# Attention on one core: ten key tiles one by one, or in five pairs, with the pair buffers in the space of W_o

## The chip, the cores and the metric

The kernel runs on one core of a Trainium2 chip. The metric is the device time of one execution in microseconds (us), as the median of the runs. Before the change three runs gave 2367.48, 2368.72 and 2373.99 us; the median is 2368.72 us.

## The reference, cut to what matters

The program is a two-layer diffusion backbone over 1024 latent tokens of width 1024. Layer 0 is grouped-query attention and a mixture of experts, layer 1 a Fourier mixer and a mixture of experts, and a final norm follows. The change touches the attention core alone:

```
k_all = concat([k_latent, k_context])            # 1024 + 256 keys
s = einsum('bqkgd,bskd->bkgqs', q, k).astype(f32) * ATTN_SCALE
p = softmax(s, axis=-1)
o = einsum('bkgqs,bskd->bqkgd', p, v)            # then o @ w_o
```

There are 16 query heads of 64, 4 key heads, and 4 query heads to a key head.

## The kernel before, in words

`phase_qkv` projects, normalises and rotates queries, keys and values. Queries lie in DRAM (`QS`), keys (`KS`, and `KL` with the low halves and two rows of ones) and values (`V`) in SBUF. `phase_attn` (L617) then works through 16 units; a unit is half of the queries (512) for one pair of heads. `phase_wo` applies W_o, and the experts follow.

`main` (L643) does one unit. For each of the ten key tiles (`kt`, 128 keys) it computes the scores of two heads: for each head one product of `KS` with `qs` (L658) and one of `KL` with `qm` (L659), which subtracts the row maximum. The scores (`st`, in PSUM, two buffers) go through the exponential on ScalarE (L673) into a tile `pe` (four buffers of 128x1024). GpSimd adds up the `pe` tiles for the softmax denominator (L680 for the first two, then L684). TensorE multiplies `pe` with V (`pv`, L664; four instructions, two for each head, each head in its own half of the output partitions), one key tile behind the scores, and accumulates in `po`. At the end ScalarE copies `po` out (L703).

Three kinds of other work are threaded in between, each as a list from which `main` pops steps:

- `fill`: the row maxima of the next unit (`smax_steps`, L548). 24 steps are a product (L561, of 512, 512 and 256 keys in turn, into two PSUM buffers `sm`) and its maximum on VectorE (L562). Then `negate` reduces, casts and subtracts on VectorE (L571, L573, L574). `fin`, always the last, transposes the result on TensorE (L581) and ScalarE copies it into `qm` (L582), which the next unit's scores need. `maxima()` pops one step, three times in each key tile, and never pops `fin`, which is popped after `pv` of tile 8.
- `tail`: the end of the unit before: `total` (four products of the sum with ones, L715, copied by L716 into `su`), four reciprocals on VectorE (L719), and `scale` (L722). One step is popped in each key tile from the third on.
- `ada`: modulation vectors of later stages. A step loads 1 MB of weights (L190, on SP's queue) and multiplies it (L245, eight instructions in four column groups of 32). It is popped in key tiles 2, 5 and 8 (`ADA_AT`), for 45 steps in all.

TensorE's instructions keep the order of the program in this phase (`manual_schedule` for PE alone). The instructions of the other engines are ordered by the planner of the framework, by its own times; a step whose inputs are ready can go ahead of its place in the program. Each engine and SP's queue then run strictly in that order.

Ahead of unit 15 (`WO_AT`) the first two quarters of W_o are loaded and split (L740: `split_piece` casts on ScalarE, L200, and subtracts on VectorE, L201) into the four 8 KB buffers of pool `wowA` (two named `wh`, two `wl`). Until then `wowA` is unused in this phase. Unit 15 has no next unit, so its `fill` is empty.

The main loop, cut:

```
for kt in range(NTA):
    scores(ps, kt, 0); maxima(); scores(ps, kt, 1)
    pe = pp.tile([P, 2, 512], F32, name="pe")
    nc.scalar.activation(pe, ps, AF.Exp, scale=SCALE)
    ...                                   # GpSimd adds pe to acc
    maxima()
    if prev is not None:
        pv(*prev)
    prev = (kt, pe)
    maxima()
    ...                                   # fin, tail, ada
pv(*prev)
```

Of the kernel before, what the change touches and what calls it, by code (L numbers as in the profile page):

```python
# [10 lines left out]
F32 = mybir.dt.float32  # L11
# [3 lines left out]
AF = mybir.ActivationFunctionType  # L15
# [5 lines left out]
P = 128  # L21
# [4 lines left out]
NTA = (SEQ + CTX) // P  # L26
# [14 lines left out]

LAG = 2
WQ_AT = 6
ADA_AT = (2, 5, 8)
SUM_DVE = (7, 8, 9)
WO_AT = 15

# [23 lines left out]
SCALE = HD ** -0.5  # L71
# [467 lines left out]
def load_queries(g, u, pool):  # L539

    hf, pr = u
    qs = pool.tile([P, 2, 512], F32R, name="qs")
    g.qs_load = g.nc.sync.dma_start(qs.bitcast(F32),
                                    g.QS[2 * pr:2 * pr + 2, :, hf * 512:(hf + 1) * 512].rearrange("h p t -> p h t"))
    return qs


def smax_steps(g, u, qs, wk, pp, tag, tagt, bufs=None):  # L548


    nc = g.nc
    hf, pr = u
    g4 = pr // 2
    m3 = g.atq.tile([P, 2, 4, 3], F32, name="m3")
    todo = []
    for h in range(2):
        for qt in range(4):
            for b, (k0, kn) in enumerate(((0, 512), (512, 512), (1024, 256))):
                def f(h=h, qt=qt, b=b, k0=k0, kn=kn):
                    ps = pp.tile([P, 512], F32, name=tag)  # L560
                    nc.tensor.matmul(ps[:, :kn], qs[:, h, qt * P:(qt + 1) * P], g.KS[:, g4, k0:k0 + kn], start=True, stop=True)  # L561
                    nc.vector.reduce_max(m3[:, h, qt, b:b + 1], ps[:, :kn], axis=AX.X)  # L562
                todo.append(f)
    qm = wk.tile([66, 2, 512], F32R, name="qm", bufs=bufs)
    nc.sync.dma_start(qm[:64].bitcast(F32), g.QS[2 * pr:2 * pr + 2, 0:64, hf * 512:(hf + 1) * 512].rearrange("h p t -> p h t"))

    box = {}

    def negate():
        nm = g.atq.tile([P, 8], F32, name="nm")  # L570
        nc.vector.tensor_reduce(nm, m3.rearrange("p h q b -> p (h q) b"), axis=AX.X, op=OP.max, negate=True)  # L571
        box["mc"] = mc = g.atq.tile([P, 8, 2], F32R, name="mc")
        nc.vector.tensor_copy(mc[:, :, 0], nm)  # L573
        nc.vector.tensor_sub(mc[:, :, 1], nm, mc[:, :, 0])  # L574

    def fin():
        mc = box["mc"]
        for h in range(2):
            pt = pp.tile([P, 512], F32R, name=tagt)
            for qt in range(4):  # L580
                nc.tensor.transpose(pt[:2, qt * P:(qt + 1) * P], mc[:, h * 4 + qt], g.identr)  # L581
            nc.scalar.copy(qm[64:66, h], pt[:2])  # L582

    todo += [negate, fin]
    return qm, todo
# [31 lines left out]
def phase_attn(g):  # L617
    nc, tc, a = g.nc, g.tc, g.a
    with ExitStack() as st:
        pp = g.pool(st, "atP", 4)  # L620
        wk = g.pool(st, "at", 2)
        third = g.pool(st, "at3", 1)
        p1 = g.pool(st, "at1", 2, psum=True)
        po_ = g.pool(st, "ato", 1, psum=True)
        p2 = g.pool(st, "at2", 2, psum=True)
        units = [(hf, pr) for g4 in range(HKV) for hf in range(2) for pr in (2 * g4, 2 * g4 + 1)]
        state = {}

        def smax(i):
            qm, todo = smax_steps(g, units[i], Q[i], wk, p1, "sm", "sm")  # L630
            state[units[i]] = (Q[i], qm)
            return todo

        def queries(i):

            if i < len(units):
                Q[i] = load_queries(g, units[i], third if i % 3 == 2 else g.atq)

        Q = {}

        tail, ada = [], []

        def main(u, fill):  # L643
            hf, pr = u
            g4 = pr // 2
            qs, qm = state.pop(u)
            po = po_.tile([P, 512], F32, name="po")
            P0 = {}
            prev = None

            def maxima(n=1):

                for _ in range(min(n, len(fill) - 1)):
                    fill.pop(0)()

            def scores(ps, kt, h):
                ks = slice(kt * P, (kt + 1) * P)
                nc.tensor.matmul(ps[:, h], g.KS[:, g4, ks], qs[:, h], start=True, stop=False)  # L658
                nc.tensor.matmul(ps[:, h], g.KL[:, g4, ks], qm[:, h], start=False, stop=True)  # L659

            def pv(kt, pe):

                for h in range(2):
                    nc.tensor.matmul(po[64 * h:64 * h + 64], g.V[:, kt, g4 * HD:(g4 + 1) * HD], pe[:, h],  # L664
                                     start=(kt == 0), stop=(kt == NTA - 1))

            for kt in range(NTA):
                ps = p2.tile([P, 2, 512], F32, name="st")
                scores(ps, kt, 0)
                maxima()  # L670
                scores(ps, kt, 1)
                pe = pp.tile([P, 2, 512], F32, name="pe")
                nc.scalar.activation(pe, ps, AF.Exp, scale=SCALE)  # L673
                side = 0 if u == units[-1] and kt in SUM_DVE else 1
                eng = (nc.vector, nc.gpsimd)[side]
                if side not in P0:
                    P0[side] = pe
                elif not isinstance(P0[side], tuple):
                    acc = wk.tile([P, 2, 512], F32, name=f"acc{side}", bufs=1 + side)
                    eng.tensor_add(acc, P0[side], pe)  # L680
                    P0[side] = (acc,)
                else:
                    acc = P0[side][0]
                    eng.tensor_add(acc, acc, pe)  # L684
                maxima()
                if prev is not None:
                    pv(*prev)
                prev = (kt, pe)
                maxima()
                if kt == NTA - 1 and fill:  # L690
                    fill.pop(0)()
                if kt >= 2 and tail:
                    tail.pop(0)()
                if kt in ADA_AT and ada:
                    ada.pop(0)()
            pv(*prev)
            if u == units[-1]:
                end = g.atq.tile([P, 2, 512], F32, name="qs")
                ou, su = end[:, 0], end[:, 1]
            else:  # L700
                ou = wk.tile([P, 512], F32, name="ou")
                su = wk.tile([P, 512], F32, name="su", bufs=1)
            nc.scalar.copy(ou, po)  # L703
            accP = P0[1][0]
            accD = P0.get(0)
            if isinstance(accD, tuple):
                accD = accD[0]


            def total():  # L710
                if accD is not None:
                    nc.gpsimd.tensor_add(accP, accP, accD)
                ps = p1.tile([P, 512], F32, name="sm")
                for h in range(2):
                    nc.tensor.matmul(ps[64 * h:64 * h + 64], g.ones64, accP[:, h], start=True, stop=True)  # L715
                nc.scalar.copy(su, ps)  # L716

            def inverse(j):
                nc.vector.reciprocal(su[:, j * P:(j + 1) * P], su[:, j * P:(j + 1) * P])  # L719

            def scale():
                nc.vector.tensor_mul(g.X[:, 4 * hf:4 * hf + 4, pr * P:(pr + 1) * P], ou.rearrange("p (t n) -> p t n", t=4),  # L722
                                     su.rearrange("p (t n) -> p t n", t=4))
            tail.extend([total] + [lambda j=j: inverse(j) for j in range(4)] + [scale])

        for l, gi in ((0, 1), (0, 2), (1, 0), (1, 1), (1, 2)):
            steps = adaln_group(g, l, gi, po_, wk, after=not ada)
            ada += steps[:-1]
            ada.append(lambda f=steps[-1], l=l, gi=gi: adaln_store(g, l, gi, f()))
        state[units[0]] = g.smax0  # L730
        queries(1)
        for i, u in enumerate(units):
            queries(i + 2)
            f1 = smax(i + 1) if i + 1 < len(units) else []
            if i == 6:
                with tc.issue_after(g.qs_load.ins):
                    for n, t in g.tab.items():
                        nc.sync.dma_start(t, a["dft_" + n])
            if i == WO_AT:
                g.wo_pieces = [split_piece(g, load_piece(g, a["attn_w_o"][0, i * 256:(i + 1) * 256], 2), g.wowA) for i in range(2)]  # L740
            with tc.manual_schedule(engines={mybir.EngineType.PE}):
                main(u, f1)
        tail.pop(0)()
        g.tail = tail
# [1367 lines left out]
```

## Time and profile before

| what | us |
|---|---|
| median of three runs | 2368.72 |
| the profiled execution | 2366.65 |
| its span, first to last instruction | 2364.70 |
| up to the attention units | about 240 |
| the sixteen units | 240 to 738.6 |
| W_o, routing, first experts' start | 738.6 to 940 |
| the rest | 940 to 2364.7 |

All times in the trace count from the start of the span. PE is TensorE's products, PEld its weight loads, DVE VectorE, ACT ScalarE, POOL GpSimd, SP the queue that issues most transfers. A row of a timeline gives start, length, engine, line, operation, tiles and how many instructions are merged in it; in brackets is how long the engine was idle before it and what ended that.

### The profile page before, as it was taken

Reading aid. Unit: us, or ns where it says so; the run is one execution under the profiler, and the core shown is the slowest. Engines: PE = TensorE matmul, PEld = TensorE weight load, DVE = VectorE, ACT = ScalarE, POOL = GpSimd, SP = SyncE. Lnnn points to the kernel's source line nnn. Section 1 sums busy time; section 2 is a strip of 40 time slices with the busy share of each in tenths; the row PEclk is TensorE's granted clock in tenths of the full one; section 3 lists DMA queues with packets and bytes.
Section 4 is the critical chain, followed back from the end, with each engine's and each line's share of the span. In section 5 each row is a group of like instructions: output and inputs, shape, how many; then the busy total and the mean of one; then the engine's idle time right before and its main releaser. Section 6 shows DMA issues by size and latency. Waiting matters only on the chain. (4 is left out here: it accounts for less than half of the span.)

```text
span 2364.7 us, 29621 instructions
## 1 busy us (share of the span) xinstructions
PE 2149.3 (91%) x10250; PEld 1424.5 (60%) x10250; DVE 1949.1 (82%) x2822; ACT 1338.1 (57%) x1741; POOL 1045.2 (44%) x560
## 2 busy tenths in 40 slices
PE   6899999999999777999999999669699999999993
PEld 3677444444445565677777766447476777776662
DVE  4878566666675788999999999676899999998995
ACT  4733344443444235677776776443476777766773
POOL 2322566676767632334334442443233434423432
PEclk8999999999999898999999999879799999999997
DMA  8544434534333777999999999645599999999995
GB/s 304 186 160 141 165 112 134 180 112 134 115 114 129 255 250 267 359 361 331 353 345 343 362 361 336 213 192 213 218 307 348 339 343 351 354 345 347 348 366 198
DMA packets 152631, 614.22 MB, mean 260 GB/s; under 512 B 26961, under 2 KB 43993, under 8 KB 106461
## 3 DMA queue, kind: packets, MB, share of 16 engines
q1 hardware_dynamic: 110188, 546.87, 63.4%
q0 software_dynamic: 24672, 54.40, 9.0%
q10 hardware_dynamic: 17616, 11.01, 1.5%
q8 instruction: 82, 1.34, 0.2%
q14 instruction: 73, 0.59, 0.1%
HBM read 559.57 MB, written 78.44 MB: 270 GB/s over the span
## 5 line engine op out<-in xcount | busy, mean ns | idle before, releaser
L207 PE MATMUL h<-wl,xh 128*104 128x512 f32 x1024 | 411.6, 402 | 20.2 <-DVE wl L1229 16.9
L206 PE MATMUL h<-wh,xh 128*104 128x512 f32 x1024 | 410.4, 401 | 3.3 <-ACT wh L1224 3.3
L208 PE MATMUL h<-wh,xl 128*104 128x512 f32 x1024 | 406.6, 397 | 0.0
L684 POOL TENSOR_TENSOR acc<-acc,pe 128x1024 f32<-128x1024 f32 x125 | 298.8, 2391 | 96.4 <-ACT pe L673 94.0
L562 DVE TENSOR_REDUCE m<-sm 128x1 f32<-128x512 f32 x360 | 206.3, 591 | 136.4 <-PE sm L561 134.7
L673 ACT ACTIVATE pe<-st 128x1024 f32<-128x1024 f32 x160 | 163.7, 1023 | 261.8 <-PE st L659 259.9
L1293 POOL DMA_INDIRECT xg<-H,idx x64 | 116.4, 1819 | 290.8 <-PE pt L1304 182.9
L207 PEld LDWEIGHTS h<-wl,xh 128*104 128x104 f32 x1024 | 173.8, 170 | 93.5 <-DVE wl L1229 28.6
L1224 ACT CAST wh<-raw 128x1024 fp32r<-128x1024 f32 x196 | 199.8, 1054 | 48.4 <-DMA raw<-in_moe_w_dram 21.2
L1229 DVE TENSOR_TENSOR wl<-raw,wh 128x1024 fp32r<-128x1024 f32 x175 | 211.1, 1245 | 12.2 <-ACT wh L1224 12.0
L1224 ACT CAST wh<-wh 128x1024 fp32r<-128x1024 f32 x180 | 185.2, 1053 | 57.2 <-DMA wh<-in_moe_w_dram 22.8
L1229 DVE TENSOR_TENSOR wl<-wh 128x1024 fp32r<-128x1024 f32 x157 | 206.3, 1336 | 11.7 <-ACT wh L1224 11.4
L206 PEld LDWEIGHTS h<-wh,xh 128*104 128x104 f32 x1024 | 173.7, 170 | 65.9 <-ACT wh L1224 4.9
L1229 DVE TENSOR_TENSOR wl<-wl,wh 128x1024 fp32r<-128x1024 f32 x163 | 206.6, 1296 | 5.7 <-ACT wh L1224 5.4
L208 PEld LDWEIGHTS h<-wh,xl 128*104 128x104 f32 x1024 | 173.4, 169 | 59.7
L1347 POOL DMA_INDIRECT Xs<-y,idx x64 | 178.0, 2781 | 70.3 <-DVE y L1346 29.3
L1224 ACT CAST wh<-wl 128x1024 fp32r<-128x1024 f32 x172 | 177.2, 1053 | 51.8 <-PE h L208 23.9
L207 PE MATMUL py<-wl,gh 128*104 128x512 f32 x512 | 204.8, 401 | 0.2 <-DVE wl L1229 0.2
L208 PE MATMUL py<-wh,gl 128*104 128x512 f32 x512 | 202.2, 397 | 0.2 <-DVE gl L1337 0.2
L206 PE MATMUL py<-wh,gh 128*104 128x512 f32 x512 | 197.5, 404 | 2.0 <-ACT gh L1336 1.8
L664 PE MATMUL po<-pe,V 128*64 128x512 f32 x640 | 174.7, 624 | 0.4 <-ACT pe L673 0.4
L1224 ACT CAST wh<-X 128x1024 fp32r<-128x1024 f32 x124 | 129.6, 1053 | 56.3 <-PE h L208 45.3
(574 smaller groups left out, 4512.6 us busy)
## 6 DMA issues: line engine op xcount, KB each, us to landing
raw<-in_moe_w_dram SPq DMA_DIRECT2D x98, 1024.0 KB
wh<-in_moe_w_dram SPq DMA_DIRECT2D x90, 1024.0 KB
wl<-in_moe_w_dram SPq DMA_DIRECT2D x86, 1024.0 KB
qs<-in_moe_w_dram SPq DMA_DIRECT2D x96, 512.0 KB
raw<-in_w_mod_dram SPq DMA_DIRECT2D x43, 1024.0 KB
X<-in_moe_w_dram SPq DMA_DIRECT2D x37, 1024.0 KB
X<-in_moe_w_dram SPq DMA_DIRECT2D x50, 512.0 KB
QS<-qst ACTq DMA_DIRECT2D x32, 256.0 KB
```

The costliest lines, as they stand in the source:

```text
L206: nc.tensor.matmul(out, lh, wh, start=start, stop=False)
L207: nc.tensor.matmul(out, lh, wl, start=False, stop=False)
L208: nc.tensor.matmul(out, ll, wh, start=False, stop=stop)
L562: nc.vector.reduce_max(m3[:, h, qt, b:b + 1], ps[:, :kn], axis=AX.X)
L664: nc.tensor.matmul(po[64 * h:64 * h + 64], g.V[:, kt, g4 * HD:(g4 + 1) * HD], pe[:, h], start=(kt == 0), stop=(kt == NTA - 1))
L673: nc.scalar.activation(pe, ps, AF.Exp, scale=SCALE)
L684: eng.tensor_add(acc, acc, pe)
L1224: nc.scalar.copy(h, t)
L1229: i = (nc.gpsimd if pool else nc.vector).tensor_sub(l, t, h)
L1293: self.last = self.g.nc.gpsimd.indirect_dma_start(out=xg, out_offset=None, in_=self.H if src is None else src, in_offset=bass.IndirectOffs ...
L1347: return y, lambda: nc.gpsimd.indirect_dma_start(out=self.X, out_offset=bass.IndirectOffsetOnAxis(ap=idx, axis=0), in_=y, in_offset=None, ...
```

## The change

The ten key tiles are taken as five pairs. A pair's exponentials go into one tile of twice the size. `pv` of a tile is put on a list `todo`; after a pair's scores all but the last two entries are popped, so that the two products with V of the pair before come one right after the other. The steps of `tail` follow them by the table `TAIL`, then one of `ada` (after pairs 1, 2, 3), then one more `maxima()`: five in a pair instead of six. In the last pair the 25th step of `fill` is popped ahead of the products and `fin` after them; the last pair's own products end the unit. In the last unit `pv` is popped tile by tile as before. The pair tiles rotate over six buffers (two in pool `atP`, two `wh`, two `wl`), and over `atP`'s two alone in unit 15, as W_o's pieces then take `wowA`.

```
-ADA_AT = (2, 5, 8)
+ADA_AT = (1, 2, 3)
+TAIL = ((), (1,), (2,), (2,), (1,))
...
-        pp = g.pool(st, "atP", 4)
+        pp = g.pool(st, "atP", 2)
...
-            for kt in range(NTA):
-                ps = p2.tile([P, 2, 512], F32, name="st")
...
+            def total_of(kt, pe):
+                side = 0 if end_ and kt in SUM_DVE else 1
...
+            def pair_tile():
+
+                if units.index(u) >= WO_AT:
+                    return pp.tile([P, 2, 2, 512], F32, name="pe")
+                g.turn += 1
+                n = g.turn % 3
+                if n == 2:
+                    return pp.tile([P, 2, 2, 512], F32, name="pe")
+                return g.wowA.tile([P, 2, 2, 512], F32, name=("wh", "wl")[n])
+
+            todo = []
+            for j in range(NTA // 2):
+                pair = pair_tile()
+                for i in range(2):
+                    kt = 2 * j + i
+                    ps = p2.tile([P, 2, 512], F32, name="st")
+                    scores(ps, kt, 0)
+                    maxima()
+                    scores(ps, kt, 1)
+                    pe = pair[:, i]
+                    nc.scalar.activation(pe, ps, AF.Exp, scale=SCALE)
+                    total_of(kt, pe)
+                    maxima()
+                    if end_ and todo:
+                        pv(*todo.pop(0))
+                    todo.append((kt, pe))
+                if j == NTA // 2 - 1 and fill:
+                    fill.pop(0)()
+                while len(todo) > (1 if end_ else 2):
+                    pv(*todo.pop(0))
+                for n in TAIL[j]:
+                    for _ in range(min(n, len(tail))):
+                        tail.pop(0)()
+                if j in ADA_AT and ada:
+                    ada.pop(0)()
+                if j == NTA // 2 - 1 and fill:
+                    fill.pop(0)()
                 maxima()
-                if prev is not None:
-                    pv(*prev)
-                prev = (kt, pe)
-                maxima()
...
-            pv(*prev)
-            if u == units[-1]:
+            while todo:
+                pv(*todo.pop(0))
+            if end_:
```

`total_of` holds the sum that stood in the loop; `end_` is true in the last unit.

## Rows read from the trace of the kernel before

**Rows 1.** Busy time by engine in the units' stretch, core 0.
```profile
core 0: us, PE busy (x) PEld busy (x) DVE busy (x) ACT busy (x) POOL busy (x), PEclk, DMA share, GB/s
240.00:738.60 498.60, 491.76 (x2149) 219.31 (x2147) 321.92 (x489) 203.49 (x227) 338.63 (x142) 0.99 0.38 128
```

**Rows 2.** The same view: a usual unit, then unit 14, then unit 15.
```profile
584.90:616.28 31.38, 30.99 (x137) 13.78 (x134) 21.34 (x33) 12.96 (x17) 21.79 (x10) 1.00 0.37 122
678.93:716.02 37.09, 33.67 (x133) 14.63 (x134) 25.63 (x35) 15.85 (x16) 24.80 (x10) 0.91 0.33 113
716.02:738.64 22.62, 22.18 (x84) 9.02 (x84) 7.00 (x7) 11.33 (x12) 15.18 (x7) 1.00 0.06 18
```

**Rows 3.** Timeline of PE in unit 15, one key tile without maxima.
```profile
724.44 0.50 PE L658 MATMUL st<-qs,KS 128*128 128x512 f32 x1
724.78 0.40 PE L659 MATMUL st<-qm,KL 66*128 66x512 f32 x1
...
725.25 0.39 PE L659 MATMUL st<-qm,KL 66*128 66x512 f32 x1
725.58 1.08 PE L664 MATMUL po<-pe,V 128*64 128x512 f32 x4
726.59 0.50 PE L658 MATMUL st<-qs,KS 128*128 128x512 f32 x1
```

**Rows 4.** The same view: two batches of the same form in a row.
```profile
720.43 1.08 PE L664 MATMUL po<-pe,V 128*64 128x512 f32 x4
721.34 1.03 PE L715 MATMUL sm<-acc,ones 128*64 128x512 f32 x4
722.30 0.50 PE L658 MATMUL st<-qs,KS 128*128 128x512 f32 x1
```

**Rows 5.** The same view in another unit: `total`, then an `ada` step.
```profile
623.80 1.08 PE L715 MATMUL sm<-acc,ones 128*64 128x512 f32 x4
624.80 1.06 PE L245 MATMUL adap<-raw,scol 128*32 128x512 f32 x8
625.80 0.50 PE L658 MATMUL st<-qs,KS 128*128 128x512 f32 x1
```

**Rows 6.** Groups of instructions, 240 to 738 us: busy, mean ns | idle before, releaser.
```profile
L684 POOL TENSOR_TENSOR acc<-acc,pe 128x1024 f32<-128x1024 f32 x125 | 298.8, 2391 | 96.4 <-ACT pe L673 94.0
L562 DVE TENSOR_REDUCE m<-sm 128x1 f32<-128x512 f32 x360 | 206.3, 591 | 136.4 <-PE sm L561 134.7
L673 ACT ACTIVATE pe<-st 128x1024 f32<-128x1024 f32 x160 | 163.7, 1023 | 261.8 <-PE st L659 259.9 <-POOL acc L684 1.9
L722 DVE TENSOR_TENSOR X<-ou,su 128x512 f32<-128x512 f32 x15 | 32.7, 2181 | 0.0
```

**Rows 7.** Timeline of all engines: the end of a unit's maxima and `fin`.
```profile
672.25 0.42 DVE L562 TENSOR_REDUCE m<-sm 128x1 f32<-128x256 f32 x1 [0.63 <-PE sm L561]
...
672.92 1.40 DVE L573 CAST mc<-nm 128x8 fp32r<-128x8 f32 x1
674.36 0.17 DVE L574 TENSOR_TENSOR mc<-nm,mc 128x8 fp32r<-128x8 f32 x1
...
677.24 0.63 PE L581 MATMUL sm<-identr,mc 128*2 128x128 f32 x8
```

**Rows 8.** The same view in unit 14: a split of W_o and what follows.
```profile
702.74 3.46 DVE L201 TENSOR_TENSOR wl<-raw,wh 128x2048 fp32r<-128x2048 f32 x1
704.76 3.67 POOL L684 TENSOR_TENSOR acc<-acc,pe 128x1024 f32<-128x1024 f32 x1 [0.71 <-ACT pe L673]
706.86 0.39 PE L561 MATMUL sm<-KS,qs 128*128 128x256 f32 x1 [2.12 <-DVE m L562]
707.98 0.48 DVE L573 CAST mc<-nm 128x8 fp32r<-128x8 f32 x1
710.57 0.63 PE L658 MATMUL st<-qs,KS 128*128 128x512 f32 x1
```

**Rows 9.** Waits of SP's queue, 240 to 738 us: in total, times, longest.
```profile
SPq L190 <- PE adap L245: 342.8, 38, 12.0
```

More of the change, by code (lines that the diff above doesn't have):

```diff
@@ L639, in phase_attn @@
         Q = {}
+        g.turn = 0
         tail, ada = [], []
@@ L648, in main @@
             P0 = {}
-            prev = None
+            end_ = u == units[-1]
             def maxima(n=1):
@@ L665, in pv @@
                                      start=(kt == 0), stop=(kt == NTA - 1))
-            for kt in range(NTA):
-                ps = p2.tile([P, 2, 512], F32, name="st")
-                scores(ps, kt, 0)
-                maxima()
[L671 to L674, printed above, removed]
+            def total_of(kt, pe):
+                side = 0 if end_ and kt in SUM_DVE else 1
                 eng = (nc.vector, nc.gpsimd)[side]
@@ L684, in main @@
                     eng.tensor_add(acc, acc, pe)
-                maxima()
-                if prev is not None:
-                    pv(*prev)
-                prev = (kt, pe)
[L689 to L695, printed above, removed]
-            pv(*prev)
-            if u == units[-1]:
+            def pair_tile():
[33 more added lines that the diff above has]
+                    fill.pop(0)()
+                maxima()
+            while todo:
+                pv(*todo.pop(0))
+            if end_:
                 end = g.atq.tile([P, 2, 512], F32, name="qs")
```

## The prediction

> **What bounds the kernel now.** I read the busy time by stretch first. In the 498.6 us of the sixteen units PE is busy for 491.8 at a granted clock of 0.99, VectorE for 322, GpSimd for 339, ScalarE for 203; the transfers use 0.38 of their engines [rows 1]. The single units say the same: a usual one takes 31.4 us with PE busy for 31.0, the others at most 21.8 [rows 2]. So this stage lasts as long as PE's list of products, and what counts is what PE's own time is made of. For that I read PE's timeline in unit 15, where no maxima stand between. A key tile lasts from 724.44 to 726.59, 2.15 us [rows 3]. Its four score products should follow each other by about 0.235 (724.78 to 725.25 is two of them), but two steps are longer: 0.34 behind the first (724.44 to 724.78) and 0.33 from the last to the products with V (725.25 to 725.58). The four instructions with V hold PE for 1.01. So each change between score products (128 output columns of the array) and products with V (two groups of 64) costs 0.10 on the way in and 0.10 on the way out.
>
> What lies behind the units waits for all heads, so I take it to move in full with their end.
>
> **The change part by part.**
>
> *Products with V side by side.* The trace has no two `pv` in a row, but a close relative: `pv` followed by `total`, both fp32 in two groups of 64. The second starts 0.91 after the first and the next score product 0.96 after it [rows 4]. One batch alone is 0.10 + 1.01 + 0.10 = 1.21; two joined are 0.10 + 0.91 + 0.96 + 0.10 = 2.07 instead of 2.42: 0.35 saved. Bounds: the 0.20 of the changes alone (nothing gained inside), and 0.35. I take 0.35, as the row has the same form. Five joins a unit in 15 units are 75 x 0.35 = 26.2 us. Unit 15 keeps its order: nothing.
>
> *`total` and `ada` behind them.* Before, `total` and the first `ada` step stand together: 0.10 + 1.00 + 1.00 + 0.10 [rows 5]. Now `total` lengthens a batch of its own form by 0.91 and `ada` by 1.00 (another form, 32 columns): 0.29 less in 14 units, 4.1 us. The second `ada` step, between maxima before, loses its 0.20 in most units, 2.9 us. The third stood behind a `pv` already. With the joins: 33.2 us, 2.2 a unit.
>
> *`negate` and `fin` closer together.* Count from the start of the 24th maximum's product. PE needs 0.12 for it, 0.10 to change and 1.87 for two `pv`, and could begin `fin` at 2.1. On VectorE the 23rd maximum ends at about 0.4, the 24th takes 0.42, then 0.2, the cast 1.40, the subtraction 0.17 [rows 7]: 2.65. Before, the subtraction ended at 674.53 and `fin` began at 677.24, with 2.7 to spare; now PE waits some 0.6. Behind `fin` stand the last two `pv`, 1.9 us, which cover ScalarE's two copies. Bounds: 0 (the cast has also taken 0.48 [rows 8]) and 1.0. I take 0.6 x 15 = 9 us given back.
>
> *Maxima more dense.* Four stand in each pair, 0.70 apart (three products of 0.235), then none for the batch of 1.9 to 3.9 us. VectorE's mean is 0.59 [rows 6], so it keeps up, as long as nothing long starts among them. It has 21.3 us of work in a unit of some 29 [rows 2], and the table puts the reciprocals and `scale` behind the batches, in VectorE's free time. But the planner may move them ahead. Bounds: 0, and one `scale` of 2.18 [rows 6] at the wrong place, 1.7 a unit after some 0.5 of slack from two buffers. I take 0.2 a unit, 3 us.
>
> *W_o.* In unit 14 the second split's subtraction took 3.46 on VectorE amid the maxima; PE stood for 2.12, after which its products took 0.63 instead of 0.40 for a while [rows 8], as at the lower of the clock's two levels (1.2 GHz); the unit's mean granted clock is 0.91. Unit 14 is 37.09, 5.7 longer than a usual one [rows 2]. The splits now need `wowA`'s buffers: the first those of a pair early in unit 14, the second the last pair's, so that it falls into unit 15, which has no maxima; VectorE is busy there for 7.0 of 22.6. ScalarE has two casts in its queue before exponentials of unit 15, and if they wait for GpSimd's sum of unit 14, PE waits for the exponentials; the sum lags by at most two adds of 2.39 [rows 6], while two `pv`, `fin` and the scores lie between. Bounds: all of the 5.7 back, or none. I take 3 back.
>
> *Buffers and queues.* Six pair tiles hold twelve key tiles instead of four; GpSimd's nine adds are 21.5 us of about 29 a unit, and ScalarE's idle time is nearly all put down to PE, 1.9 us of it to GpSimd [rows 6]. In unit 15 two tiles hold four key tiles as before, though freed two at a time: bounds 0 and the 1.9, taken as 0. On SP's queue nothing is added; each 1 MB load waits for the `ada` step three before it, 38 waits [rows 9], so it is issued about a unit early, and moving the steps to pairs 1 to 3 leaves that lead near 29 us. Nothing.
>
> **The sum**: -33.2 + 9 + 3 - 3 = -24.2 us against the profiled execution's own 2366.65, 2.07 below the median: **2342.4 us**.
>
> **The rivals.**
>
> *A. VectorE's long steps fall among the dense maxima.* For it: the planner takes what is ready: W_o's splits, placed ahead of unit 15, ran within unit 14 [rows 8]. If it starts just before a pair's four maxima, each of 14 units loses 1.7 more: 24 us, all of the gain. Against it: the table leaves gaps of 2.9 us and longer (two `pv` and an `ada` step) right behind the reciprocals' places. Time: 2366.
>
> *B. The drain stays.* If two `pv` in a row don't flow into each other as `pv` and `total` do (both write the same `po`, which no row shows), a join saves 0.20: 75 x 0.15 less, and 2 less for `total`. Time: 2356.
>
> *C. Slower: `scale` gets ahead of `negate` on VectorE.* Then the cast starts 2.2 us later, and PE stands at `fin` for 2.8 instead of 0.6 in each of 14 units. Only `fin` decides: from a wait of 2.2 us on, a unit is longer than before. Time: 2342.4 + 14 x 2.2 = 2373; more if PE's clock then falls as in unit 14. Against it: in program order `negate` comes first, and `scale` is ready a pair earlier. The cast itself speaks for such delays: 1.40 in one unit [rows 7] and 0.48 in unit 14 [rows 8], for the same 8 columns. The Trainium skill ("SBUF — State Buffer", section "SBUF: two separate sides") says that VectorE and GpSimd share a port pair under an exclusive lock, so that the later one blocks for a whole instruction. So the cast waits for the add then running, and as a pair's adds now come back to back, it could wait for two. The rows agree so far: the cast of 707.98 ends at 708.46, just behind the add that ends at 708.43 [rows 8]. By that rule the wait at `fin` would be up to 2.4 more, the same time as rival C's.
>
> **How the numbers follow.** My forecast gets 0.62, A 0.17, B 0.10, C 0.11. Low end: no new waits and all of W_o's loss back, -33.2 - 5.7, 2328; high end: A with a usual wait, 2367. That leaves C and a tail of each side out. A difference under 0.3% (7 us) can't be told from none. Faster by more: the forecast, B and a small part of A, 0.76. Within: most of A, 0.13. Slower: C, 0.11.
>
> **What would show it.** After the change a usual unit should take 29.4 to 29.8 us. Right: with nothing of `tail` or `ada` behind two `pv`, the next score or maximum product starts 1.87 after them (2.02 by B); `fin` with an idle PE of 0.5 to 0.7 ahead of it, put down to VectorE's `mc`; unit 14 below 35; W_o's second split inside unit 15. Wrong: idle PE time put down to L562's maxima over 1 us a unit (A); `fin` waiting for over 2 us, or `scale` between the 24th maximum and the cast (C); a longer stretch behind the units than before, for the move in full.

## The result, and the profile after

The changed kernel takes **2330.34 us** (median of four runs, 2329.97 to 2331.77), against 2368.44 us for the kernel before, measured with it (2367.48 to 2373.99). The ratio is 0.9835, with a 95% interval of 0.9818 to 0.9853: 38.1 us faster. The forecast was 24.2 us faster. A second measurement of the two kernels (e10, among the experiments) gave 2337.16 and 2368.15, 31.0 us faster.

First the profile by stretch. A unit is taken to end where ScalarE starts to copy `po` out. The busy times below are those of the kernel before, in units 1 to 13 and in all that follows the units; then of the changed kernel, in all units, in a usual one, in units 1 to 13, in unit 14, in unit 15 and behind them. The columns are those of [rows 1].

```profile
274.37:678.93 404.56, 402.26 (x1789) 179.80 (x1790) 273.19 (x420) 161.90 (x183) 278.23 (x118) 1.00 0.38 127
738.64:2364.70 1626.06, 1452.92 (x7096) 1054.73 (x7096) 1458.11 (x1881) 1018.77 (x1255) 636.27 (x325) 0.95 0.88 310
```

```profile
240.00:705.59 465.59, 455.09 (x2146) 228.92 (x2143) 303.93 (x489) 202.97 (x227) 342.15 (x142) 0.99 0.41 137
535.64:565.15 29.51, 28.99 (x141) 14.57 (x142) 19.01 (x32) 12.46 (x14) 21.84 (x9) 1.00 0.42 135
271.93:653.05 381.12, 373.80 (x1789) 188.90 (x1790) 254.15 (x420) 162.04 (x182) 283.64 (x117) 1.00 0.40 135
653.05:681.94 28.89, 28.23 (x133) 14.43 (x134) 23.17 (x34) 14.15 (x16) 21.70 (x9) 1.00 0.16 55
681.94:705.59 23.65, 22.15 (x84) 9.01 (x84) 11.08 (x9) 13.01 (x14) 15.45 (x7) 1.00 0.32 105
705.59:2328.20 1622.61, 1452.23 (x7096) 1053.93 (x7096) 1455.02 (x1881) 1018.08 (x1255) 644.65 (x325) 0.95 0.88 310
```

PE is still what bounds the units. Units 1 to 13 lose 23.44 us (404.56 to 381.12), 1.80 each, with the same 1789 PE instructions. PE's busy time falls by 28.46, 2.19 a unit, and its idle time grows from 2.30 to 7.32, 0.39 a unit. By the same marks unit 0 and what precedes it lose 2.44 (end at 274.37, now 271.93), unit 14 falls from 37.09 [rows 2] to 28.89 and unit 15 grows from 22.62 to 23.65. At the end of the units 33.05 us are gained (738.64 to 705.59); the other 3.45 of the span's 36.5 lie behind them, where no code changed.

PE's timeline shows where its busy time went: two `pv` (eight instructions), `total` and `ada` in one chain, then two `pv` with nothing behind.

```profile
571.08 1.94 PE L666 MATMUL po<-pe,V 128*64 128x512 f32 x8
572.85 1.03 PE L740 MATMUL sm<-acc,ones 128*64 128x512 f32 x4
573.80 1.07 PE L246 MATMUL adap<-raw,scol 128*32 128x512 f32 x8
574.80 0.50 PE L562 MATMUL sm<-KS,qs 128*128 128x512 f32 x1
...
583.79 1.94 PE L666 MATMUL po<-wl,V 128*64 128x512 f32 x8
585.66 0.50 PE L562 MATMUL sm<-KS,qs 128*128 128x512 f32 x1
```

Two `pv` take 1.77 up to `total` (0.91 each would be 1.82 [rows 4]), `total` 0.95, and from two `pv` to the next product of 128 columns it is 1.87.

The timeline of all engines at the end of a unit's maxima, which answers to [rows 7]:

```profile
559.95 4.83 POOL L680 TENSOR_TENSOR acc<-acc,wl 128x1024 f32<-128x1024 f32 x2 [0.55 <-ACT wl L702]
560.14 1.94 PE L666 MATMUL po<-wh,V 128*64 128x512 f32 x8
560.93 1.41 DVE L574 CAST mc<-nm 128x8 fp32r<-128x8 f32 x1
562.37 0.17 DVE L575 TENSOR_TENSOR mc<-nm,mc 128x8 fp32r<-128x8 f32 x1
562.59 0.64 PE L582 MATMUL sm<-identr,mc 128*2 128x128 f32 x8 [0.52 <-DVE mc L575]
```

`fin` (L582) now waits, 0.52 here. The groups of instructions of all units (columns as in [rows 6]) say how often and how long:

```profile
L574 DVE CAST mc<-nm 128x8 fp32r<-128x8 f32 x15 | 21.8, 1452 | 0.5
L747 DVE TENSOR_TENSOR X<-ou,su 128x512 f32<-128x512 f32 x15 | 16.2, 1083 | 0.0
L582 PE MATMUL sm<-identr,mc 128*2 128x128 f32 x120 | 9.6, 222 | 8.4 <-DVE mc L575 8.4
```

PE idles 8.4 us ahead of 15 `fin`, 0.56 each. No other wait of PE in units 1 to 13 is put down to VectorE; before, there were four for a maximum, 1.2 us together. `scale` (L747) is down from a mean of 2181 ns [rows 6] to 1083.

Last the seam of units 14 and 15, the timeline that answers to [rows 8]:

```profile
676.12 1.89 ACT L201 CAST wh<-raw 128x2048 fp32r<-128x2048 f32 x1
...
679.53 4.18 DVE L202 TENSOR_TENSOR wl<-raw,wh 128x2048 fp32r<-128x2048 f32 x1 [0.20 <-issue]
682.42 1.91 ACT L201 CAST wh<-raw 128x2048 fp32r<-128x2048 f32 x1
684.23 1.94 ACT L702 ACTIVATE pe<-st 128x1024 f32<-128x1024 f32 x2
685.30 1.08 PE L666 MATMUL po<-pe,V 128*64 128x512 f32 x4 [1.35 <-ACT pe L702]
```

Both of W_o's subtractions (L202) are out of unit 14's maxima, and the clock there stays at its upper level (granted 1.00, before 0.91). But the second cast stands on ScalarE ahead of unit 15's first exponentials, and PE waits 1.35 for them.

### The profile page after: what moved, and what is told of

It reads as the page before. It is cut to its first block, busy times and chain, and to the rows that moved or that the text cites. A ratio compares the mean times of both kernels' runs of the same rounds, so it can differ in the third digit from the quotient of the medians.

```text
span 2328.2 us, 29541 instructions
## 1 busy us (share of the span) xinstructions
PE 2109.7 (91%) x10250; PEld 1431.8 (61%) x10250; DVE 1927.7 (83%) x2822; ACT 1337.7 (57%) x1741; POOL 1057.2 (45%) x560
## 5 line engine op out<-in xcount | busy, mean ns | idle before, releaser
L1254 POOL TENSOR_TENSOR wl<-wh 128x1024 fp32r<-128x1024 f32 x23 | 68.5, 2978 | 172.0 <-ACT wh L1249 151.5
L1254 DVE TENSOR_TENSOR wl<-X,wh 128x1024 fp32r<-128x1024 f32 x113 | 139.1, 1263 | 4.9 <-ACT wh L1249 4.8
L562 PE MATMUL sm<-KS,qs 128*128 128x512 f32 x360 | 135.4, 383 | 0.0
```

Of the source, the lines that this page charges most:

```text
L1254: i = (nc.gpsimd if pool else nc.vector).tensor_sub(l, t, h)
```

## The experiments

Three theories were to be told apart. **Order**: PE gains because products of one form follow each other. **Buffers**: six pair tiles instead of four single ones let the engines run freely. **W_o**: what was gained came mostly from the splits leaving unit 14. The table has each kernel's stages in its one profiled execution, and the median of its runs with their range; on the three chips of the experiments the kernel before had medians of 2366.49, 2367.01 and 2368.15. The ratio is to the kernel before on the same chip. "Behind" runs from the end of the units to the end of the span.

| kernel | units 1 to 13, each | unit 14 | unit 15 | behind | median (range), us | ratio, 95% interval |
|---|---|---|---|---|---|---|
| before | 31.12 | 37.09 | 22.62 | 1626.06 | 2368.44 (2367.48 to 2373.99) | |
| changed | 29.32 | 28.89 | 23.65 | 1622.61 | 2330.34 (2329.97 to 2331.77) | 0.9835 (0.9818 to 0.9853) |
| e1_single | 31.44 | 31.53 | 29.29 | 1626.75 | 2370.58 (2368.39 to 2381.63) | 1.0024 (1.0002 to 1.0045) |
| e2_wo_late | 31.11 | 30.66 | 27.06 | 1628.73 | 2366.63 (2359.57 to 2373.04) | 0.9999 (0.9988 to 1.001) |
| e3_two_bufs | 29.38 | 34.50 | 22.31 | 1633.87 | 2340.55 (2339.27 to 2346.35) | 0.9887 (0.9871 to 0.9904) |
| e4_early_max | 32.73 | 31.17 | 28.70 | 1632.43 | 2387.91 (2385.8 to 2392.29) | 1.0086 (1.0069 to 1.0103) |
| e5_three_before_fin | 28.68 | 28.16 | 23.65 | 1627.92 | 2327.27 (2324.22 to 2332.05) | 0.9829 (0.9799 to 0.9859) |
| e6_apart | 31.08 | 30.82 | 23.64 | 1623.72 | 2360.96 (2357.91 to 2367.47) | 0.9974 (0.9957 to 0.999) |
| e7_last_pairs | 29.32 | 28.91 | 23.43 | 1628.01 | 2334.36 (2331.28 to 2338.93) | 0.9856 (0.9825 to 0.9886) |
| e8_all | 28.68 | 28.13 | 20.81 | 1634.53 | 2328.04 (2323.22 to 2330.21) | 0.9822 (0.9793 to 0.9851) |
| e10_after_again | 29.31 | 28.83 | 23.65 | 1628.91 | 2337.16 (2336.56 to 2341.18) | 0.9874 (0.9853 to 0.9896) |
| e11_three_again | 28.68 | 28.11 | 23.65 | 1621.88 | 2327.21 (2320.82 to 2330.8) | 0.9829 (0.9808 to 0.9851) |
| e9_three_late_cast | 28.69 | 28.10 | 22.49 | 1628.22 | 2324.95 (2321.72 to 2333.52) | 0.9828 (0.9804 to 0.9853) |

The stages inside the units repeat to 0.1 us where their code is the same (units 1 to 13 of the changed kernel, e7 and e10). The stretch behind them doesn't: it lies between 1621.88 and 1634.53. So a cause is read here from the stages, and the medians say whether it survives to the end.

### One key tile at a time, in the changed kernel's buffers (e1_single)

```diff
-                    if end_ and todo:
+                    if todo:
                         pv(*todo.pop(0))
                     todo.append((kt, pe))
-                if j == NTA // 2 - 1 and fill:
-                    fill.pop(0)()
-                while len(todo) > (1 if end_ else 2):
-                    pv(*todo.pop(0))
+                    maxima()
...
-                maxima()
```

> The changed kernel with its products with V popped tile by tile again (one batch behind each tile's scores, three maxima in a tile, as before the change); six pair buffers, TAIL, ADA_AT and the place of W_o stay. Theory (the joined products pay): five joins of 0.35 a unit are lost, the wait of 0.58 at fin goes, so a unit takes about 30.5 us instead of 29.3, and the whole 2330 + 15 x 1.2 = 2348 us, in a range of 2343 to 2353. Rival (more buffers and the maxima's spacing pay, not the order): units stay near 29.3 and the whole within 4 us of 2330.

Measured: units of 31.44, and a ratio of 1.0024 (1.0002 to 1.0045). With the pair tiles but without the pairs' order all of the gain is gone, so **Order** holds and **Buffers** falls. A unit was expected at 30.5, from the five joins alone. The busy times of units 1 to 13 show what that left out:

```profile
272.04:680.73 408.69, 403.99 (x1789) 180.72 (x1790) 258.78 (x420) 162.07 (x182) 278.85 (x118) 1.00 0.38 126
```

PE is busy for 31.08 a unit, so what `total` and `ada` had gained is gone too, and it idles 0.36. Besides, unit 15 takes 29.29 at a granted clock of 0.88. The timeline there:

```profile
715.28 1.90 ACT L201 CAST wh<-raw 128x2048 fp32r<-128x2048 f32 x1 [2.43 <-POOL acc L680]
717.09 1.93 ACT L702 ACTIVATE pe<-st 128x1024 f32<-128x1024 f32 x2
...
718.16 1.59 PE L666 MATMUL po<-pe,V 128*64 128x512 f32 x4 [4.09 <-ACT pe L702]
```

The second cast waits for the buffer until GpSimd has added the last `pe` that lies in it, the exponentials wait behind the cast, PE stands for 4.09, and its next products take 1.59 instead of 1.08. In the changed kernel the same place cost 1.35.

### The kernel before, with W_o's splits behind unit 14 (e2_wo_late)

The edit is on the kernel before.

```diff
-            nc.scalar.copy(ou, po)
+            g.ou = nc.scalar.copy(ou, po).ins
...
-                g.wo_pieces = [split_piece(g, load_piece(g, a["attn_w_o"][0, i * 256:(i + 1) * 256], 2), g.wowA) for i in range(2)]
+                with tc.issue_after(g.ou):
+                    g.wo_pieces = [split_piece(g, load_piece(g, a["attn_w_o"][0, i * 256:(i + 1) * 256], 2), g.wowA) for i in range(2)]
```

> The kernel before, with W_o's first two splits held on ScalarE behind the copy that ends unit 14. Theory (in unit 14 they blocked VectorE amid the maxima and then slowed PE's clock): unit 14 goes from 37.1 to about 31.1 us, unit 15 gets 1 us longer as exponentials wait behind the casts, the whole loses 5 us: 2363, in a range of 2361 to 2365. Rival (unit 14 is long for another reason, its last ada loads or the clock by itself): unit 14 stays over 35 us and the whole within 2 us of the kernel before.

Measured: unit 14 falls by 6.43 to 30.66, 0.45 below the mean of units 1 to 13. So the splits had cost it all that it stood out by. But unit 15 grows by 4.44, where 1 was expected, and no difference can be seen in the total (0.9999, 0.9988 to 1.001). The timeline at its start:

```profile
708.79 3.70 ACT L200 CAST wh<-raw 128x2048 fp32r<-128x2048 f32 x2
...
712.39 1.94 ACT L673 ACTIVATE pe<-st 128x1024 f32<-128x1024 f32 x2
...
713.47 1.75 PE L664 MATMUL po<-pe,V 128*64 128x512 f32 x4 [3.13 <-ACT pe L673]
```

Two casts in a row, 3.70, stand ahead of the exponentials; PE idles 3.13 and then runs slower (1.75 for a `pv` of 1.08). **W_o** alone therefore doesn't make the gain: moved as a whole the cost goes from VectorE in unit 14 to ScalarE in unit 15. The changed kernel moves one of the two casts only, and pays 1.03.

### Two pair tiles throughout, `wowA` left free for W_o (e3_two_bufs)

```diff
-                if units.index(u) >= WO_AT:
+                if True:
                     return pp.tile([P, 2, 2, 512], F32, name="pe")
```

> The changed kernel with the two pair buffers of pool atP alone in all units, wowA left free as in the kernel before. Theory (a pair's products end two pairs ahead and GpSimd lags by at most two adds, so two buffers are enough): units 1 to 13 stay at 29.3 us; W_o's splits go back into unit 14 amid the maxima and cost 5 to 8 us there: 2335 to 2338. Rival (the six buffers are needed): exponentials wait for GpSimd's adds, units lengthen by 0.3 us or more each, the whole is 2342 or more.

Measured: 29.31 for each of units 1 to 12, as with six tiles (29.30). So the four tiles in `wowA` buy nothing in a usual unit. Unit 14 is 34.50, 5.6 longer than in the changed kernel, at a granted clock of 0.95. The timeline shows W_o's first cast at the end of unit 13, and then the old picture again:

```profile
652.11 1.90 ACT L201 CAST wh<-raw 128x2048 fp32r<-128x2048 f32 x1
...
653.92 0.58 ACT L728 COPY ou<-po 128x512 f32<-128x512 f32 x1
...
663.99 3.96 DVE L202 TENSOR_TENSOR wl<-raw,wh 128x2048 fp32r<-128x2048 f32 x1 [2.28 <-ACT wh L201]
...
668.60 0.38 PE L562 MATMUL sm<-KS,qs 128*128 128x256 f32 x1 [2.08 <-DVE m L563]
...
670.00 0.62 PE L562 MATMUL sm<-KS,qs 128*128 128x512 f32 x1
```

The first cast delays the copy that marks the end of unit 13, so that unit counts 0.8 too much and unit 14 as much too little. The two together take 6.4 more than in the changed kernel, and unit 15 takes 1.3 less (22.31). So the place of W_o is worth 5.1 us at the end of the units (710.73 here, 705.59 in the changed kernel). The whole, 2340.55, lies above the 2335 to 2338 expected, with a long stretch behind the units (1633.87). What the shared buffers are worth is the dependence: a split can't start before the last pair tile in its buffer is used up.

### Two maxima at the end of each pair, none late (e4_early_max)

```diff
-                if j == NTA // 2 - 1 and fill:
-                    fill.pop(0)()
                 while len(todo) > (1 if end_ else 2):
                     pv(*todo.pop(0))
...
-                maxima()
+                maxima(2)
```

> The changed kernel with two maxima instead of one at the end of each pair, so that all 24 and negate are done before the last pair's products. Theory (PE's wait of 0.58 at fin is the only new wait): it goes, 0.58 x 15 = 8.7 us, and the whole is 2322, in a range of 2320 to 2325. Rival (denser maxima make PE wait for VectorE as much elsewhere): 2328 to 2332, with the wait put down to L562's maxima.

Measured: the wait at `fin` is gone, as meant, but a unit takes 32.73, 3.41 more, and the kernel is slower than before (1.0086, 1.0069 to 1.0103). The waits of PE (in total, times, longest) from 274 to 640 us, and a timeline:

```profile
PE sm L562 <- DVE m L563: 25.2, 34, 1.6
```

```profile
582.81 2.70 DVE L745 TENSOR_TENSOR X<-ou,su 128x512 f32<-128x512 f32 x1
...
586.17 0.50 PE L562 MATMUL sm<-KS,qs 128*128 128x512 f32 x1 [1.55 <-DVE m L563]
...
587.38 0.63 PE L660 MATMUL st<-qs,KS 128*128 128x512 f32 x1
```

This is the prediction's rival A, at more than its price of 1.7 a unit: `scale` starts right ahead of three maxima, both `sm` buffers fill, PE stands, and then its products take 0.63 instead of 0.40. One more maximum behind each of the first four pairs, four in a unit, decides between 29.3 and 32.7 us.

### Three `pv` ahead of `fin`, one behind (e5_three_before_fin)

```diff
-                while len(todo) > (1 if end_ else 2):
+                while len(todo) > (1 if end_ or j == NTA // 2 - 1 else 2):
```

> The changed kernel with three products with V ahead of fin and one behind it, instead of two and two. Nothing else moves; VectorE's list is the same. Theory (PE waits 0.56 at fin in each unit for negate's chain, and only for that): the third product covers it, 0.56 x 15 = 8.4 us, the whole is 2322, in a range of 2319 to 2325. Rival (the wait only moves, to the copies of qm behind fin, which one product with V of 1.0 no longer covers): 2328 to 2332.

Measured: 28.68 a unit, 0.64 less, and no wait at `fin`. The wait at `fin` was 0.56 of it, and 0.08 is PE's busy time (372.77 in units 1 to 13, before this edit 373.80). The ratio is 0.9829 (0.9799 to 0.9859).

### A maximum between the two `pv` (e6_apart)

```diff
                 while len(todo) > (1 if end_ else 2):
                     pv(*todo.pop(0))
+                    if j < NTA // 2 - 1 and len(todo) == 3:
+                        maxima()
...
-                maxima()
+                if j == 0:
+                    maxima()
```

> The changed kernel with the maximum that stood at the end of pairs 1, 2 and 3 put between the two products with V there: as many maxima in each pair, same buffers, same W_o, and only the two products no longer adjoin. Theory (an interrupted join costs 0.35, 0.20 for the change of form and 0.15 of drain): 3 x 0.35 x 15 = 16 us, units of 30.4 instead of 29.3, the whole 2346, in a range of 2343 to 2349. Rival B of the prediction (adjoining saves only the change of form, 0.20): 9 us, 2339. Rival (order does not matter): 2330.

Measured: 31.08 a unit, 1.76 more, so three interrupted joins take nearly all of the gain away (0.9974, 0.9957 to 0.999). The timeline at one of them, and further on in the same unit:

```profile
590.68 1.08 PE L666 MATMUL po<-pe,V 128*64 128x512 f32 x4
591.69 0.49 PE L562 MATMUL sm<-KS,qs 128*128 128x512 f32 x1
592.12 1.08 PE L666 MATMUL po<-pe,V 128*64 128x512 f32 x4
593.03 1.03 PE L743 MATMUL sm<-acc,ones 128*64 128x512 f32 x4
...
601.01 2.04 DVE L750 TENSOR_TENSOR X<-ou,su 128x512 f32<-128x512 f32 x1
...
604.31 0.39 PE L562 MATMUL sm<-KS,qs 128*128 128x256 f32 x1 [0.58 <-DVE m L563]
```

From the first `pv` to `total` are 2.35 (590.68 to 593.03). In the changed kernel it is 1.77, and a product of 128 columns and 512 keys takes 0.235 among others of its form [rows 3], 2.00 together: the interruption costs 0.35, the value that the prediction took for a join. Three are 1.04 a unit. The other 0.7 are not the joins. By PE's start times, 0.58 of them lie between a score product and the maximum's product behind it (71.0 us of units 1 to 13, in the changed kernel 63.6): PE comes late there, as at 604.31, where VectorE had taken up `scale` at 601.01, just ahead of maxima. The two shares were not separated by a run of their own.

### The last unit in pairs as well (e7_last_pairs), and with all of it together (e8_all)

```diff
-                    if end_ and todo:
-                        pv(*todo.pop(0))
...
-                while len(todo) > (1 if end_ else 2):
+                while len(todo) > 2:
```

> The changed kernel with pairs in the last unit too (its products with V are popped tile by tile in the change). Theory: four or five joins of 0.35 in unit 15, which goes from 23.65 to about 22 us; the whole 2328.5, in a range of 2326 to 2330. Rival (in the last unit exponentials, or GpSimd's sum with two pair buffers, are late): unit 15 does not shorten.

Measured: unit 15 takes 23.43 instead of 23.65, and the total shows no gain (2334.36, between the 2330.34 and 2337.16 of the changed kernel). PE still waits 1.35 behind the cast, and here its clock falls (granted 0.93 in unit 15; the changed kernel's 1.00): the first two `pv` take 3.32 instead of 1.94. These 1.38 are nearly all that four or five joins should have brought. Why the clock fell after this wait, and not after the same wait in the changed kernel, is open.

e8 joins this with three `pv` ahead of `fin` and a second cast that comes behind unit 15's second exponential:

```diff
-                    nc.scalar.activation(pe, ps, AF.Exp, scale=SCALE)
+                    ex = nc.scalar.activation(pe, ps, AF.Exp, scale=SCALE).ins
+                    if end_ and kt == 1:
+                        with tc.issue_after(ex):
+                            g.wo_pieces.append(split_piece(g, g.wo_raw, g.wowA))
...
```

> The changed kernel with three edits together: three products with V ahead of fin, pairs in the last unit, and W_o's second split held on ScalarE behind the second exponential of unit 15 (there PE waited 1.35 us for an exponential behind that cast). Theory: 8.4 + 1.7 + 1.3 us less: 2319, in a range of 2316 to 2323. Rival (the stretch behind the units, which starts with W_o, gets longer by what the units get shorter): 2326 to 2331.

Measured: the units end 11.7 us earlier than in the changed kernel, at 693.87, and unit 15 is down to 20.81. The total is 2328.04, no better than e5 on the same chip (2327.27). The timeline shows what is late next:

```profile
690.75 1.94 ACT L702 ACTIVATE pe<-st 128x1024 f32<-128x1024 f32 x2 [3.30 <-POOL acc L680]
...
698.96 1.98 PE L741 MATMUL sm<-acc,ones 128*64 128x512 f32 x4 [5.14 <-POOL acc L738]
```

With only two pair tiles ScalarE waits for GpSimd's adds, and `total` of the last unit waits 5.14 for the sum of denominators. It starts at 698.96, only 0.5 ahead of its start in e5 (699.50), though the units end 2.9 earlier than there (693.87 and 696.78). So what e8 gains in unit 15 over e5 is given back, but for 0.5, right behind the units.

### The change once more, three `pv` again, and the late cast alone (e10, e11, e9)

The three ran on one chip, five runs each. e10 is the changed kernel itself, e11 is e5, e9 is e5 with the late cast of e8.

> The changed kernel itself once more, beside the next two on one chip. Theory (what stands behind the units is not shortened by the change; its 1622.6 us there were one end of a spread of some us between runs and chips): the stretch behind the units is 1622 to 1630 and the ratio to the kernel before between 0.983 and 0.987. Rival (the change shortens it by 3.5 us): 1622 to 1624 again.

> Three products with V ahead of fin and one behind, once more, for a comparison on one chip. Theory: units of 28.7 instead of 29.3 us, so 9 us less than the changed kernel beside it, as far as the stretch behind the units is the same for both. Rival (that stretch takes it back): within 4 us of it.

> Three products with V ahead of fin, and W_o's second cast held on ScalarE behind the second exponential of unit 15; the last unit tile by tile as in the change. Theory (PE waited 1.35 us in unit 15 for an exponential behind the cast): unit 15 goes from 23.65 to about 22.4, 1.3 us less than with three products alone. Rival (the cast then delays the third exponential by as much): unit 15 stays over 23.3.

Measured: e11 is 9.95 us faster than e10 (2327.21 and 2337.16; no run of the one reaches a run of the other), where 13 units of 0.63 and unit 14's 0.72 make 8.9. e9's unit 15 falls by 1.16 to 22.49, but its median of 2324.95 can't be told from e11's. The busy time of units 1 to 13 in e11, then of the stretch behind the units in e10:

```profile
272.47:645.36 372.89, 372.88 (x1789) 188.81 (x1790) 254.20 (x420) 162.05 (x182) 283.63 (x118) 1.00 0.41 138
```

```profile
705.90:2334.80 1628.90, 1452.27 (x7096) 1055.79 (x7096) 1449.57 (x1881) 1018.09 (x1255) 622.21 (x325) 0.95 0.88 309
```

In e11 PE is busy for 372.88 of 372.89 us: in this order nothing is left to wait for. So three `pv` ahead of `fin` beat the change, with or without the late cast. In e10 the units end 0.31 us later than in the first profile of the changed kernel, while the stretch behind them takes 6.3 us more. The ratio of e10 lies just outside the 0.983 to 0.987 expected, its stretch behind the units inside the 1622 to 1630.

## Why the prediction was right, point by point

The direction and its mechanism were right, and the measured time lies inside the range, near its low end. By its own steps, at the end of the units (forecast -24.2, measured -33.05):

- **Joins, `total` and `ada`: right.** 2.2 a unit were forecast, and PE's busy time fell by 2.19. e6 prices one join at 0.35, so rival B's 0.20 (the drain stays) is refuted, as 1.87 behind two `pv` also says. The rows fit a page of the Trainium skill ("TensorEngine Tiling (Array Packing)", section "Key Properties"), which says that changing the tiling mode drains TensorE.
- **`fin`: right.** Forecast an idle 0.6 put down to VectorE's `mc`, measured 0.56; e5 shows that nothing else hangs on it. (VectorE's terms as listed there add up to 2.59, not 2.65; at this size it changes nothing.)
- **"Maxima more dense": the size was off, with the sign.** The step took 0.2 a unit as a loss. PE's other idle time, 2.30 us in units 1 to 13 before, is gone instead: 0.18 a unit gained. Over units 1 to 13 this 0.38 makes 4.9 of the 5.1 us by which they beat the forecast. The step counted four maxima from batch to batch, where there are five, and rested on a `scale` of 2.18; that takes half as long now (last section). Whether the shorter `scale` is why the idle time went, no run shows. Rival A was real, but in e4, not here: in the change, in the unit whose `pv` are shown, `scale` starts at 584.74, beside the two of 583.79, while PE asks VectorE for nothing.
- **"W_o": mis-sized.** 3 were taken from bounds of 0 and 5.7. Unit 14 was 5.97 above the mean of units 1 to 13 and is now 0.43 below it, as it is in e2 by 0.45: 6.40 back. Of this 1.03 are lost again in unit 15, in the casts' place that the step had named, but not by a wait for GpSimd's sum: the one cast there takes 1.91 and starts without a wait. Nor was the first split early in unit 14, as the step had it: its cast ran at 676.12, and its subtraction behind the last maximum. Net 5.4, 2.4 more than forecast; e3 puts it at 5.1. e2 and e1 show how near the rest lay: with both casts late 4.44 of 6.43 are lost again, and with one that waits for GpSimd, in e1, all.
- **"Buffers and queues": right at nothing** for a usual unit (e3), and unit 15's 1.03 belongs to W_o's cast: e9, which moves the cast alone, takes 1.16 off.
- **Unit 0**, counted as any other unit at 1.4, gave 2.44. Why was not tried; 1.2 may be spread, as e2, whose unit 0 is that of the kernel before, ends it at 273.16 instead of 274.37.
- **The move in full: right as far as the spread lets one see.** That stretch took 3.45 us less than before in the first profile of the changed kernel and 2.9 more in e10; so the 3.45 can't be put down to the change, and neither can the 2.9.
- **Rival C was not seen**: in all 14 units that have both, `scale` starts 4.9 to 6.9 us ahead of the cast (554.03 and 560.93 in the unit shown), and `fin`'s longest wait is 0.7.

So about 9 us of the gap between forecast and measurement at the end of the units come from the maxima (5.3 in units 1 to 14), W_o in units 14 and 15 (2.4) and unit 0 (1.0); the rest of the first measurement is spread of the code behind, and the second gives the change 0.9874 (0.9853 to 0.9896). The three misses point the same way, so none hid another. That the second median, 2337.16, lies only 5.2 us below the forecast is luck of that spread: its units end where those of the first profile do.

## What to carry to other kernels

Where TensorE bounds a stage, price each change between forms of product from PE's timeline, and group batches of one form. Then count what the regrouping makes dense for the engine that consumes the results: the same maxima in a slightly different place made the kernel slower than at the start (e4). When a block of background work is moved, look at each engine that it uses: W_o's split is a cast on one engine and a subtraction on another, and only one of them was in the way in unit 14, the other in unit 15.

## What the runs showed of the hardware that was not expected

Some instructions of VectorE wait inside their own time for GpSimd's instruction beside them; the maxima don't (592 ns, before 591 [rows 6]). `scale` in the kernel before, then in the changed one (timelines of both engines):

```profile
603.25 2.37 POOL L684 TENSOR_TENSOR acc<-acc,pe 128x1024 f32<-128x1024 f32 x1 [0.34 <-ACT pe L673]
603.92 2.25 DVE L722 TENSOR_TENSOR X<-ou,su 128x512 f32<-128x512 f32 x1
```

```profile
554.03 0.68 DVE L747 TENSOR_TENSOR X<-ou,su 128x512 f32<-128x512 f32 x1
554.08 5.32 POOL L680 TENSOR_TENSOR acc<-acc,wh 128x1024 f32<-128x1024 f32 x2 [1.03 <-ACT wh L702]
```

Started 0.67 behind an add, `scale` ends 0.55 behind that add's end; started just ahead of one it takes 0.68, and the two adds take 5.32 instead of 4.83. `scale` takes 0.68 in nine of the fifteen units, and 16.5 us of VectorE's time vanish (15 times 2181 less 1083 ns) without a line of it changed. The cast of 128x8 elements does the same: 1.41 at 560.93, up to the end of the first of the two adds beside it, and in e4, where GpSimd had been idle for 1.03 up to 562.19, 0.17:

```profile
561.20 0.17 DVE L574 CAST mc<-nm 128x8 fp32r<-128x8 f32 x1
561.41 0.17 DVE L575 TENSOR_TENSOR mc<-nm,mc 128x8 fp32r<-128x8 f32 x1
562.19 2.36 POOL L680 TENSOR_TENSOR acc<-acc,pe 128x1024 f32<-128x1024 f32 x1 [1.03 <-ACT pe L702]
```

The Trainium skill ("SBUF — State Buffer", section "SBUF: two separate sides") calls the shared port pair an exclusive lock, held for a whole instruction; all these rows agree.

The other surprise is the spread: the kernel before, unchanged, ran between 2360.78 and 2381.23 us on these chips, and the stretch behind the units differs by 6 us between two profiles of one and the same kernel (1622.61 and 1628.91 for the change, 1627.92 and 1621.88 for e5 and e11, on two chips). What sets it was not tried.
